# Weaving the top-k selection into the first half's query projection as well

## The chip, the cores and the metric

One core of one Trainium2 chip runs one layer of a streaming encoder in float32. The metric is the time of one execution on the device in microseconds (us). Engines in what follows: PE is TensorE (matmuls and transposes), DVE VectorE, ACT ScalarE, POOL GpSimd, SP the SyncE queue, which issues all the DMAs that this text speaks of.

## The reference, cut to what matters

The layer normalises 2048 prompt rows and 128 sample rows (17 tiles of 128 rows; tile 16 is the sample), multiplies them by one wide input matrix, and sends the columns to two mixers: a gated spatial mixer, and a sparse attention. For the sparse attention every query row first scores all keys with an indexer, keeps the 256 best, and attends to those alone:

```python
def _sparse_attend(q, qi, wi, q_pos, k, v, kidx, k_pos, topk):
    rel = jax.nn.relu(jnp.einsum('bqhd,bld->bqhl', qi, kidx) * (IDX_DIM ** -0.5))
    score = jnp.einsum('bqhl,bqh->bql', rel, wi).astype(jnp.float32) * (N_IDX_HEADS ** -0.5)
    score = jnp.where(_chunk_mask(q_pos, k_pos)[None], score, -jnp.inf)
    top_val, top_idx = lax.top_k(score, topk)
    ...
    p = jax.nn.softmax(logits, axis=-1).astype(v.dtype)
    out = jnp.einsum('bqhgn,bqnhd->bqhgd', p, v_sel)
```

The mixers' results are gated, projected, added to the input and normalised once more.

## The kernel before, in words

**Stages.** The 17 tiles are two halves, tiles 0 to 8 and 9 to 16, each of three groups of up to three tiles. The program goes through these stages:

1. `phase_p1(0)`: of half 0 the projections to keys, values and indexer keys (row by row, 128x292 matmuls), then to the indexer's queries (`C_QI`), then to the attention's queries (`C_Q`), both as 128x384 matmuls with the results stored to DRAM (`qi_s`, `q_s`, line 316).
2. `turn` of half 1 (normalised rows transposed into `hh` and `hl`), then `phase_p1(1)`, the same for half 1.
3. `phase_p2(1)`: the spatial mixer and the merge gates of half 1, and then, after the `turn` back, `phase_p2(0)` for half 0. Its last DVE instruction is a product at line 508.
4. `phase_b`: the attention, tile by tile from 0 to 15. DVE subtracts the penalty of unselected keys from the logits and takes the maximum (line 741), ACT takes the exponential, PE transposes, ACT and DVE split the transposed probabilities into two parts (lines 179 and 182), PE multiplies them with the values (line 780). Woven in at a low rate are the sample's attention (`attend_sample`, which takes over the selection's SBUF) and the first half of the merge (`merge_early`).
5. `phase_c`: the rest of the merge, the output projection and the last norm.

All float32 products are made of three products of a high and a low part (line 173), so PE has much to do everywhere; the weights' low part is a subtraction on POOL (line 182, `wl`).

**The selection.** `select(t, lane)` makes one tile's penalty. `scores` loads the tile's indexer queries (lines 518 and 519), multiplies them with the indexer keys on PE (lines 537 and 538), and adds up the eight heads on ACT and DVE (lines 540 to 544). A bisection over 31 bits then looks for the 256th score: each step counts how many of the tile's L scores are at least a candidate, in even and odd steps by turns on DVE (line 614) and on ACT as a sum of signs (line 624), and moves the candidate with two tiny DVE instructions (lines 625 or 629, and 630). At its end it goes over the scores in chunks of 512 (lines 656 to 663) and stores the penalty to DRAM (line 665). L is 128 times (t + 1): the last tiles are the dearest. Two lanes of tiles run beside each other, lane 0 with tiles 0, 1, 3, 5, 7, 9, 11, 13, 15 and lane 1 with 2, 4, 6, 8, 10, 16, 12, 14.

**What sets the order.** Each stage is a generator that yields the cost of what it has just emitted (`feats` yields 24 * n / 2400 for n columns). `weave(main, back, rate)` emits the main stage, and for each unit of cost lets `back` emit `rate` units: 0.95 for the selection in stages 2 and 3, 0.15 in `phase_b`. What is left of the selection is emitted at `drain(back)`, before the attention. The order in which each engine then gets its instructions is made when the program is built: a scheduler plays the program through and moves what it takes to be ready ahead of what it takes to be late, within the dependencies. On the chip each engine's list is fixed. The lines that call the stages:

```python
    drain(phase_p1(0, hT, p1, wa, lambda: nxt.ahead(4)))
    back = lanes(chain(select_all_of([0, 1]), *(select(t, 0) for t in (3, 5, 7, 9, 11, 13, 15))),
                 chain(*(select(t, 1) for t in (2, 4, 6, 8, 10, 16, 12, 14))))
    ...
    back = weave(phase_p1(1, hT, p1, wa), back, 0.95)
```

Of the kernel before, what the change touches and what calls it, by code (L numbers as in the profile page):

```python
# [36 lines left out]
C_U, C_V, C_ZA, C_Q, C_K, C_VV, C_ZB, C_QI, C_KI, C_WI, C_GA, C_GB = (  # L37
    0, 512, 1024, 1536, 2048, 2304, 2560, 3072, 3584, 3648, 3656, 4680)
# [3 lines left out]
GROUP_OF = {t: (g, i) for g, ts in enumerate(GROUPS) for i, t in enumerate(ts)}  # L42
# [15 lines left out]
def encoder_step(ctx: ExitStack, tc: tile.TileContext, x_prompt, x_sample, cache_k, cache_v, cache_kidx,  # L58
# [24 lines left out]
    class Banks:  # L83
# [4 lines left out]
        def set(self, **n):  # L88
            if self.pool:
                self.pool.close()  # L90
            self.n = n
            self.pool = Pool("ps_" + "_".join(n), space=bass.MemoryType.PSUM) if n else None
# [118 lines left out]
    def cols(c, n=256):  # L211
        return w_in[0][:, c:c + n]
# [60 lines left out]
    def phase_p1(half, hT, p1, wa, at_queries=None):  # L273

        gs = HALVES[half]
        gids = [GROUP_OF[g[0]][0] for g in gs]

        wb = load_w([cols(C_KI + 36, 36), cols(C_VV)], True)
        for gid, g in zip(gids, gs):
            k2s = []  # L280
            for i, t in enumerate(g):
                kk = p1.tile([P, 584], F32, tag="kk", name="kk", bufs=3)
                for j, w in enumerate((wa, wb)):
                    pk = bank("mm")
                    yield from rows(hT, pk[:, :292], t, w, 0, 292)
                    nc.scalar.activation(kk[:, 292 * j:292 * (j + 1)], pk[:, :292], AF.Copy)
                ST.dma_start(out_rows(o_k, s_k, t, "s h d -> s (h d)"), kk[:, :256])
                ST.dma_start(out_rows(o_ki, s_ki, t, None), kk[:, 256:320])
                ST.dma_start(out_rows(o_v, s_v, t, "s h d -> s (h d)"), kk[:, 328:])
                nc.vector.tensor_scalar(wiw[:, t, :], kk[:, 320:328], float(H ** -0.5) * 2.0 ** 24, None, op0=OP.mult)  # L290
                if t < NPT:
                    k2 = p1.tile([P, 2, HD], F32, tag="k2", name="k2", bufs=3)
                    nc.vector.tensor_copy(k2, kk[:, None, 256:320].to_broadcast([P, 2, HD]))
                    k2s.append(k2)
                else:
                    PS.dma_start(wi_s, wiw[:, t, :])
            m, c0 = len(k2s) * P, g[0] * P
            tp = bank("tr")
            for i, k2 in enumerate(k2s):
                nc.tensor.transpose(tp[:, i * P:(i + 1) * P], k2.rearrange("p a d -> p (a d)"), ident)  # L300
            split_hi(kist[:, c0:c0 + m], tp[:, :m])
            split_lo(kist[HD:, c0:c0 + m], tp[HD:, :m], kist[HD:, c0:c0 + m])
        for c, dst in ((C_QI, qi_s), (C_Q, q_s)):
            for b in range(2):
                if at_queries and c == C_Q and b:
                    at_queries()
                w = load_w([cols(c + 256 * b)])
                for j in range(2):
                    for gid in gids:
                        n = len(GROUPS[gid]) * P  # L310
                        pq = bank("mm")
                        yield from feats(hT, pq[:, :n], gid, w, j * P)
                        sb = p1.tile([P, 384], F32, tag="ev", name="ev", bufs=3)
                        nc.scalar.activation(sb[:, :n], pq[:, :n], AF.Copy)
                        r = (2 * b + j) * P
                        ST.dma_start(dst[gid][r:r + P, :], sb[:, :n])

    AT_FROM = 1

# [280 lines left out]

    def select(t, lane):

        keys = ("scores",) if t < NPT else ("scores", "mask")
        yield from take(*keys)
        s, L = yield from (scores(t) if t < NPT else scores_sample(lane))
# [28 lines left out]
        nxt = tk.tile([P, 1], F32, tag=f"bd{lane}", name="nxt")  # L634
# [427 lines left out]
    def chain(*gens):  # L1062
        for g in gens:
            yield from g
# [17 lines left out]
    def weave(main, back, rate):  # L1082

        due = 0.0
        for c in main:
            due += c * rate
            while due > 0.0 and back is not None:
                try:
                    due -= next(back)
                except StopIteration:  # L1090
                    back = None
        return back

    def drain(back):
        for _ in back or ():
            pass
# [4 lines left out]
    p1 = Pool("p1")  # L1101
    first = Normed(0, p1, 4).ahead(1)
    wa = load_w([cols(C_K), cols(C_KI, 36)], True, None, p1)
    hT = first.turn()
    nxt = Normed(1, p1, 4, first.gbc)
    drain(phase_p1(0, hT, p1, wa, lambda: nxt.ahead(4)))
    back = lanes(chain(select_all_of([0, 1]), *(select(t, 0) for t in (3, 5, 7, 9, 11, 13, 15))),
                 chain(*(select(t, 1) for t in (2, 4, 6, 8, 10, 16, 12, 14))))
    wa = load_w([cols(C_K), cols(C_KI, 36)], True)
    hT = nxt.turn()  # L1110
    back = weave(phase_p1(1, hT, p1, wa), back, 0.95)
# [8 lines left out]
    hT = px[1].turn()  # L1120
# [62 lines left out]
```

## Time and profile before

| | |
|---|---|
| three runs | 2234.58, 2236.76 and 2247.63 us, median 2236.76 us |
| profiled execution | 2242.49 us, of which the span from the first to the last instruction is 2240.7 us |
| granted PE clock, mean of the span | 0.978 of 2.4 GHz |
| busy share of the span | PE 96%, PE weight loads 91%, DVE 71%, ACT 54%, POOL 27% |
| stages in the span | `phase_p1(0)` to about 185 us, `phase_p1(1)` to 360, `phase_p2` to 1400, `phase_b` to 1986, `phase_c` to the end |
| selection | its first count starts at 203.3 us, its last chunk at 1555.6 us |

The busy time of PE is made of records whose ends are modelled, each longer than the distance to the next one, so a PE that shows as busy throughout can still be given more work in a stretch; the number of matmuls in a stretch is therefore read beside it. The granted clock of a stretch is 1.00 where the clock stood at 2.4 GHz throughout, and less where part of the stretch ran at 1.2 GHz.

### The profile page before, as it was taken

The page shows a single profiled execution, that of the slowest core. Times are in us where ns is not written, and L with a number is a line of the kernel's source. Part 1 is how long each engine was busy: PE and PEld are TensorE (multiplying, and loading weights), DVE is VectorE, ACT ScalarE, POOL GpSimd, SP SyncE. Part 2 cuts the span into 40 slices and gives each one's busy share as a digit, 9 for nine tenths or more (in the row PEclk, how much of TensorE's full clock was granted, in tenths as well). Part 3 has the DMA queues.
Part 4 walks back from the last instruction along what each step waited for, and adds up shares of the span by engine and source line. Part 5 has one row for each costly group of instructions (what it writes and reads, how often), then busy time and mean ns, then how long its engine had stood idle before and what let it go on. Part 6 is the DMA issues. An engine that isn't in the chain of part 4 may idle for free. (4 is left out here: it accounts for less than half of the span.)

```text
span 2240.7 us, 38226 instructions
## 1 busy us (share of the span) xinstructions
PE 2144.5 (96%) x13896; PEld 2030.0 (91%) x13896; DVE 1588.7 (71%) x4057; ACT 1215.8 (54%) x2181; POOL 594.8 (27%) x693
## 2 busy tenths in 40 slices
PE   8999999999999999999999999588999999998998
PEld 7999999999999998999999999577988999987886
DVE  7105857988897797856787678899788677755443
ACT  6225646565764655346664455776677666552221
POOL 1221222232432231222243221233212544333000
PEclk9999999999999999999999999699999999999999
DMA  6233233223432233112142211433332544244342
GB/s 209 80 109 114 82 96 95 68 67 87 129 105 83 73 108 104 48 59 90 40 136 85 82 56 54 118 80 89 92 79 53 145 122 117 88 153 145 130 160 76
DMA packets 251006, 218.83 MB, mean 98 GB/s; under 512 B 46529, under 2 KB 238657, under 8 KB 250817
## 3 DMA queue, kind: packets, MB, share of 16 engines
q1 hardware_dynamic: 250816, 216.39, 32.9%
q8 instruction: 109, 1.79, 0.3%
q14 instruction: 81, 0.66, 0.1%
HBM read 152.45 MB, written 63.81 MB: 97 GB/s over the span
## 5 line engine op out<-in xcount | busy, mean ns | idle before, releaser
L182 POOL TENSOR_TENSOR wl<-ws,wh 128x256 fp32r<-128x256 f32 (+1 forms) x376 | 310.7, 856 | 915.7 <-ACT wh L179 903.7
L624 ACT ACTIVATE junk<-s,bc 128x384 int8<-128x384 f32 (+14 forms) x232 | 294.0, 1268 | 185.5 <-DVE bc L630 184.0
L173 PE MATMUL ps_mm<-wh,hl 128*128 128x256 f32 (+1 forms) x1360 | 392.7, 289 | 0.9 <-DVE hl L182 0.9
L173 PE MATMUL ps_mm<-wh,hh 128*128 128x256 f32 (+1 forms) x1360 | 391.9, 289 | 1.5 <-ACT wh L179 0.7
L173 PE MATMUL ps_mm<-wl,hh 128*128 128x256 f32 (+1 forms) x1360 | 390.7, 287 | 0.3 <-POOL wl L182 0.3
L173 PE MATMUL ps_mm<-hh,wh 128*128 128x384 f32 (+1 forms) x1152 | 378.9, 329 | 2.4 <-ACT ev L474 2.4
L173 PE MATMUL ps_mm<-hl,wh 128*128 128x384 f32 (+1 forms) x1152 | 378.7, 329 | 0.0
L173 PE MATMUL ps_mm<-hh,wl 128*128 128x384 f32 (+1 forms) x1152 | 377.7, 329 | 0.0
L614 DVE TENSOR_SCALAR_CACHE_REDUCE junk<-s,bc 128x512 int8<-128x512 f32 (+14 forms) x248 | 351.9, 1421 | 5.2
L173 PEld LDWEIGHTS ps_mm<-wh,hh 128*128 128x128 f32 x1360 | 259.0, 191 | 6.1 <-issue 1.7
L173 PEld LDWEIGHTS ps_mm<-wh,hl 128*128 128x128 f32 x1360 | 259.1, 191 | 4.2 <-DVE hl L182 1.2
L173 PEld LDWEIGHTS ps_mm<-wl,hh 128*128 128x128 f32 x1360 | 259.3, 191 | 2.2 <-POOL wl L182 0.5
L544 DVE SCALAR_TENSOR_TENSOR s<-r,wiw,s 128x384 f32<-128x384 f32 (+2 forms) x266 | 201.5, 774 | 65.0 <-ACT r L540 64.2
L173 PEld LDWEIGHTS ps_mm<-hh,wh 128*128 128x128 f32 x1152 | 217.9, 189 | 4.6 <-ACT ev L474 2.8
L173 PEld LDWEIGHTS ps_mm<-hl,wh 128*128 128x128 f32 x1152 | 217.7, 189 | 2.1
L173 PEld LDWEIGHTS ps_mm<-hh,wl 128*128 128x128 f32 x1152 | 217.8, 189 | 1.8
L540 ACT ACTIVATE r<-ps_ix 128x512 f32<-128x512 f32 (+2 forms) x304 | 157.2, 538 | 111.3 <-PE ps_ix L538 104.7
L763 PE MATMUL ps_tr<-ident,sx 128*128 128x128 f32 x1088 | 177.0, 281 | 14.8 <-ACT sx L746 4.3
L780 PE MATMUL ps_po<-pth,vst 128*128 128x256 f32 x544 | 161.7, 313 | 9.3 <-ACT osb L784 8.8
L182 DVE TENSOR_TENSOR ptl<-ps_tr,pth 128x512 fp32r<-128x512 f32 (+1 forms) x231 | 149.6, 658 | 28.7 <-ACT pth L179 27.7
L179 ACT ACTIVATE pth<-ps_tr 128x512 fp32r<-128x512 f32 (+1 forms) x231 | 127.6, 572 | 76.4 <-PE ps_tr L763 69.7
L746 ACT ACTIVATE sx<-sx,mx 128x128 f32<-128x128 f32 (+15 forms) x128 | 153.6, 1201 | 20.6 <-DVE mx L745 20.2
(287 smaller groups left out, 4572.7 us busy)
## 6 DMA issues: line engine op xcount, KB each, us to landing
ws<-in_w_in_dram SPq DMA_DIRECT2D x88, 512.0 KB, 3.9
x<-in_x_prompt_dram SPq DMA_DIRECT2D x41, 512.0 KB, 3.6
q<-q_s SPq DMA_DIRECT2D x34, 256.0 KB, 4.4
out_dram<-x SPq DMA_DIRECT2D x17, 512.0 KB, 2.6
gb_s<-ev SPq DMA_DIRECT2D x40, 192.0 KB, 2.5
ma_s<-ev SPq DMA_DIRECT2D x40, 192.0 KB, 1.9
ma<-ma_s SPq DMA_DIRECT2D x40, 192.0 KB, 3.3
sg<-gb_s SPq DMA_DIRECT2D x40, 192.0 KB, 2.4
```

The costliest lines, as they stand in the source:

```text
L173: nc.tensor.matmul(out, a(k), b(k), start=(n == 0), stop=(n == 3 * nk - 1))
L179: nc.scalar.activation(dst, src, AF.Copy)
L182: (eng or nc.vector).tensor_tensor(dst, src, hi.bitcast(F32), op=OP.subtract)
L540: nc.scalar.activation(r[:, :n], pi[:, :n], AF.Relu, scale=HD ** -0.5)
L544: nc.vector.scalar_tensor_tensor(s[:, c:c + n], r[:, :n], wiw[:, t, h:h + 1], s[:, c:c + n], op0=OP.mult, op1=OP.add)
L614: nc.vector.tensor_scalar(junk[:, :L], s[:, :L], thr, 0.0, op0=op, op1=OP.add, accum_out=cnt)
L624: nc.scalar.activation(junk[:, :L], s[:, :L], AF.Sign, bias=candf, scale=-1.0, accum_out=cnt)
L746: nc.scalar.activation(sx, sx, AF.Exp, bias=mx[:, 7:8], scale=HD ** -0.5, accum_out=T.rsum[:, h:h + 1])
L763: nc.tensor.transpose(tv[:, l, hh * P:(hh + 1) * P], pr[hh][:, (l0 + l) * P:(l0 + l + 1) * P], ident)
L780: nc.tensor.matmul(po, vst[:, l0 + l, n, :], pp[:, l, :], start=(l0 + l == 0 and i == 0), stop=(l0 + l == t and i == 1))
```

## The change

The selection's generator is made before `phase_p1(0)` instead of after it, and that stage is woven with it at 0.95 too. `weave` gives `back` no turn until some indexer queries have been emitted in full: at the end of the `C_QI` block the half's three groups enter `asked`, and until `asked` holds something nothing is due. A tile whose group is not yet in `asked` waits in `select`, each turn of waiting counted as 0.5. Nothing else is changed, and the same instructions are issued. From line 318 on the lines of the changed kernel are five higher than before, from line 603 on seven.

```diff
                         r = (2 * b + j) * P
                         ST.dma_start(dst[gid][r:r + P, :], sb[:, :n])
+            if c == C_QI:
+                asked.update(gids)
+
+
+    asked = set()
 
     AT_FROM = 1
...
     def select(t, lane):
 
+        while GROUP_OF[t][0] not in asked:
+            yield 0.5
         keys = ("scores",) if t < NPT else ("scores", "mask")
...
         due = 0.0
         for c in main:
-            due += c * rate
+            due += c * rate if asked else 0.0
             while due > 0.0 and back is not None:
...
     nxt = Normed(1, p1, 4, first.gbc)
-    drain(phase_p1(0, hT, p1, wa, lambda: nxt.ahead(4)))
     back = lanes(chain(select_all_of([0, 1]), *(select(t, 0) for t in (3, 5, 7, 9, 11, 13, 15))),
                  chain(*(select(t, 1) for t in (2, 4, 6, 8, 10, 16, 12, 14))))
+    back = weave(phase_p1(0, hT, p1, wa, lambda: nxt.ahead(4)), back, 0.95)
     wa = load_w([cols(C_K), cols(C_KI, 36)], True)
```

How it moves instructions is seen at two places. The first is DVE where the projections end, from the last product of `phase_p2(0)` (line 508 before, 513 in the changed kernel). Before, the list goes on like this (`bn` is the count, `bg` and `bc` the step and the candidate, `eq`, `pre` and `pen` the chunks, 128x1920 the scores of tile 14):

```order
L508 TENSOR_TENSOR ev<-ev,ps_mm 128x384
L659 COPY bl<-pre 128x1
L661 SCALAR_TENSOR_TENSOR eq<-pre,bd,eq 128x512
L625 TENSOR_SCALAR bg<-bn 128x1
L663 SCALAR_TENSOR_TENSOR pen<-junk,eq 128x512
L630 SCALAR_TENSOR_TENSOR bc<-bg,bc 128x1
L656 TENSOR_SCALAR eq<-s,bc 128x512
L614 TENSOR_SCALAR junk,bn<-s,bc 128x1920
L657 SCALAR_TENSOR_TENSOR pre<-eq,bl 128x512
L629 TENSOR_SCALAR bg<-bn 128x1
```

The changed kernel's DVE list at the same place, where `kst` and `q` are already the attention's first keys and queries:

```order
L513 TENSOR_TENSOR ev<-ev,ps_mm 128x384
L636 TENSOR_SCALAR bg<-bn 128x1
L637 SCALAR_TENSOR_TENSOR bc<-bg,bc 128x1
L632 TENSOR_SCALAR bg<-bn 128x1
L637 SCALAR_TENSOR_TENSOR bc<-bg,bc 128x1
L621 TENSOR_SCALAR junk,bn<-s,bc 128x1920
L636 TENSOR_SCALAR bg<-bn 128x1
L637 SCALAR_TENSOR_TENSOR bc<-bg,bc 128x1
L632 TENSOR_SCALAR bg<-bn 128x1
L637 SCALAR_TENSOR_TENSOR bc<-bg,bc 128x1
L621 TENSOR_SCALAR junk,bn<-s,bc 128x1920
L182 TENSOR_TENSOR kst<-ps_tr,kst 64x4x128
```

Tile 15's last chunks no longer stand there. Counted to the end of the selection, 88 DVE instructions of the selection come behind that product before and 52 in the changed kernel: of the counts 12 and 6, of the steps 20 and 9, of the chunks 6 and 4; on ACT 10 sums of signs and 4. The last chunk stands behind 79 of the attention's subtractions of line 741 before, behind 45 in the changed kernel.

The second place is the SP queue in `phase_p1(0)`, where the `C_Q` results (`q_s`, three groups) are stored and the next stage's weights (`ws`) are loaded. Before:

```order
L316 DMA q_s_80<-ev 128x384
L316 DMA q_s_78<-ev 128x384
L316 DMA q_s_79<-ev 128x384
L316 DMA q_s_80<-ev 128x384
L157 DMA ws<-in_w_in_dram 128x4x256
L316 DMA q_s_78<-ev 128x384
L157 DMA ws<-in_w_in_dram 128x4x36
L316 DMA q_s_79<-ev 128x384
L157 DMA ws<-in_w_in_dram 128x4x36
L316 DMA q_s_80<-ev 128x384
L157 DMA ws<-in_w_in_dram 128x4x256
L316 DMA q_s_78<-ev 128x384
```

In the changed kernel, a little further on in the same stage:

```order
L316 DMA q_s_78<-ev 128x384
L316 DMA q_s_79<-ev 128x384
L157 DMA ws<-in_w_in_dram 128x4x36
L157 DMA ws<-in_w_in_dram 128x4x256
L523 DMA qi<-qi_s_85 64x8x128
L524 DMA qi<-qi_s_85 64x8x128
L316 DMA q_s_80<-ev 128x384
L316 DMA q_s_78<-ev 128x384
L316 DMA q_s_79<-ev 128x384
L228 DMA x<-in_x_prompt_dram 128x1024
L316 DMA q_s_80<-ev 128x384
```

The indexer queries of tiles 3 and 4 are now loaded between the stores of `C_Q`; before, the queue carried one such load there, that of tile 2 ahead of the `C_Q` stores, and the next came in `phase_p1(1)`. On PE the first product of line 537 moves from the row numbered 1045 to the row numbered 758, into `C_Q` of half 0, and the last from 8587 to 8372.

## Rows read from the trace of the kernel before

**Rows 1.** The page: busy time of each engine, and two rows of 40 slices.
```profile
PE 2144.5 (96%) x13896; PEld 2030.0 (91%) x13896; DVE 1588.7 (71%) x4057; ACT 1215.8 (54%) x2181; POOL 594.8 (27%) x693
...
PE   8999999999999999999999999588999999998998
...
PEclk9999999999999999999999999699999999999999
```

**Rows 2.** Windows: length, busy PE, PEld, DVE, ACT, POOL (instructions), clock, DMA share, GB/s.
```profile
80.00:160.00 80.00, 80.00 (x467) 79.96 (x466) 2.57 (x4) 18.26 (x30) 23.64 (x34) 1.00 0.36 106
...
280.00:300.00 20.00, 17.44 (x93) 17.11 (x93) 10.71 (x24) 7.19 (x16) 7.12 (x8) 0.83 0.38 111
...
320.00:340.00 20.00, 20.00 (x127) 20.00 (x126) 13.54 (x44) 11.62 (x26) 3.16 (x5) 1.00 0.23 70
...
800.00:880.00 80.00, 75.26 (x505) 70.47 (x504) 67.47 (x149) 40.67 (x61) 18.61 (x23) 0.96 0.38 116
...
1280.00:1360.00 80.00, 80.00 (x447) 78.41 (x446) 62.14 (x114) 45.47 (x69) 16.25 (x20) 1.00 0.23 67
...
1600.00:1760.00 160.00, 157.13 (x1091) 141.72 (x1090) 129.14 (x385) 115.23 (x222) 42.10 (x45) 0.99 0.31 78
```

**Rows 3.** Windows at the attention's start.
```profile
1400.00:1411.00 11.00, 1.59 (x7) 1.25 (x8) 9.57 (x19) 4.15 (x6) 1.16 (x1) 0.58 0.77 186
...
1411.00:1498.00 87.00, 65.77 (x377) 58.01 (x375) 74.72 (x249) 69.79 (x166) 26.48 (x28) 0.78 0.36 90
1498.00:1560.00 62.00, 52.53 (x355) 47.44 (x354) 58.73 (x168) 39.63 (x82) 15.16 (x14) 0.94 0.29 74
```

**Rows 4.** Windows of line 614 (DVE) and line 624 (ACT), accumulator reads included.
```profile
1400.00:1560.00 160.00, 26.59 (x24) 0.83 0.36 90
...
1400.00:1560.00 160.00, 17.82 (x18) 0.83 0.36 90
```

**Rows 5.** DVE's groups from 1411 to 1560: busy, mean ns | idle before.
```profile
L614 DVE TENSOR_SCALAR_CACHE_REDUCE junk<-s,bc 128x1920 int8<-128x1920 f32 x9 | 19.9, 2208 | 0.1
...
L630 DVE SCALAR_TENSOR_TENSOR bc<-bg,bc 128x1 int32<-128x1 int32 x17 | 6.1, 358 | 0.1
...
L661 DVE SCALAR_TENSOR_TENSOR eq<-pre,bd,eq 128x512 f32<-128x512 f32 x3 | 3.1, 1037 | 0.0
L657 DVE TENSOR_TENSOR_SCAN pre<-eq,bl 128x512 f32<-128x512 f32 x2 | 2.6, 1276 | 0.0
...
L663 DVE SCALAR_TENSOR_TENSOR pen<-junk,eq 128x512 bf16<-128x512 int8 x3 | 2.0, 678 | 0.0
L656 DVE TENSOR_SCALAR eq<-s,bc 128x512 f32<-128x512 f32 x3 | 1.4, 477 | 0.0
L629 DVE TENSOR_SCALAR bg<-bn 128x1 int32<-128x1 f32 x9 | 1.3, 147 | 0.1
```

**Rows 6.** PE's longest wait from 1400 to 1560: us in total, times, longest.
```profile
PE ps_tr L699 <- DMA kk<-out_dram: 11.5, 2, 7.1
```

**Rows 7.** Timeline of DVE: 45th subtraction, next count, the selection's last chunk.
```profile
1492.06 0.56 DVE L741 CUSTOM_DVE_ANT_0 sx<-ps_mm,pen 128x384 f32<-128x384 f32 x1
...
1493.03 2.21 DVE L614 TENSOR_SCALAR_CACHE_REDUCE junk<-s,bc 128x1920 int8<-128x1920 f32 x1
...
1555.57 0.56 DVE L663 SCALAR_TENSOR_TENSOR pen<-junk,eq 128x384 bf16<-128x384 int8 x1
```

**Rows 8.** Timeline of PE: the stalls near the selection's start, idle in brackets.
```profile
208.44 0.50 PE L537 MATMUL ps_ix<-kist,qih 128*128 128x512 f32 x1 [2.52 <-ACT qih L179]
...
293.07 0.69 PE L537 MATMUL ps_ix<-kist,qih 128*128 128x384 f32 x1 [2.56 <-ACT r L540]
```

**Rows 9.** POOL's weight splits: 80 to 130 (ns min/median/max), then 260 to 360.
```profile
L182 POOL TENSOR_TENSOR wl<-ws,wh x24: 727/737/751, 80.1 to 121.8; 128x256 fp32r<-128x256 f32 x24
...
L182 POOL TENSOR_TENSOR wl<-ws,wh 128x256 fp32r<-128x256 f32 x34 | 27.0, 823 | 59.6 <-ACT wh L179 59.6
```

**Rows 10.** Waits of the SP queue over the span: total, times, longest.
```profile
SPq L518 <- PE ps_ix L538: 33.5, 9, 17.5
```

## The prediction

> **What bounds the kernel now.** I read the page first [rows 1]. PE is busy for 96% of the span, no other engine for more than 71%, and the row of slices has one hole: the 26th slice (1400 to 1456 us) shows 5 tenths, the two behind it 8. The granted clock falls to 0.6 in the same slice. So nearly all of the kernel waits for PE, whose work this change doesn't touch, and what can be won lies in that hole.
>
> The windows show how the stages differ. In the projections PE is full, whether the selection runs beside them or not (80 to 160 us without it, 320 to 340 and 1280 to 1360 with it) [rows 2]. In the steady attention it is full too: 157.1 of 160 us with 1091 matmuls, DVE at 129.1 (1600 to 1760) [rows 2]. Only at the attention's start is DVE the fuller engine [rows 3]: 58.7 of 62 us (95%) from 1498 to 1560, where PE has 52.5, and 74.7 of 87 from 1411 to 1498, where PE has 65.8. The first 11 us there are something else: PE waits for the first keys [rows 6], and DVE is busy with leftover selection.
>
> That selection ends at 1556 us [rows 7], 156 us after the projections, and it sits in the same in-order DVE list as the attention's subtractions. From 1400 to 1560 its counts take 26.6 us of DVE and its sign sums 17.8 us of ACT [rows 4], and beside the counts stand steps and chunks [rows 5]. So this is the stage to price.
>
> **The change, part by part.** All instructions stay; they move.
>
> *Start in the first half.* The 12 products of half 0's `C_Q` yield 24 * 384 / 2400 = 3.84 each, 46.1 in all, so the selection is emitted 0.95 * 46.1 = 44 units sooner. In time it is 12 * 24 = 288 matmuls at 80 us / 460 = 174 ns (nearly all the 467 records of that window are these): 50 us [rows 2]. DVE was busy for 2.6 of 80 us there and ACT for 18.3, so the work fits beside PE. PE's own part of it (lines 537 and 538) is only moved: what it adds in this stage it takes from later ones, and its sum is zero, since PE is full in both. No tile waits for `asked` later: summing the yields, half 1's `C_QI` is out after 127 units of selection, and lane 0 comes to tile 9, the first of that half, after 237.
>
> *New stalls, or stalls that go.* The selection's start costs PE something now: 2.52 us idle at 208, 2.56 us at 293 with the clock at 0.83 over 20 us (another 3.4 us) [rows 2, 8]. That is 8.5 us that may vanish, since DVE and ACT are emptier where it starts now. On the other side, the `turn` of half 1 had DVE and ACT nearly to itself and now meets counts. The nearest row is the second `turn`, inside the woven selection: 4.7 us idle and a clock of 0.96 (3.2 us), 8 us (800 to 880) [rows 2]. Between -8.5 and +8 I take 0: one is as near as the other.
>
> *POOL.* A weight split takes 737 ns while DVE is idle and 823 ns beside the selection [rows 9]. Some 24 splits come in the newly woven stretch (eight for the last `C_Q` weights, eight for each of the next two): 24 * 86 ns = 2 us. POOL is busy for 30% there [rows 2], so this is covered by its idle time; without that cover it is 2 us. The Trainium skill (GPSIMD Engine Reference, Key points) has GpSimd share its SBUF interfaces with VectorE, in contention above all with two-input DVE instructions. By that rule alone the change would cost these 2 us; the trace agrees on the contention (737 against 823 ns).
>
> *The end of the projections.* By the changed order, 6 counts, 11 steps and 2 chunks of DVE leave the attention's start, and 6 sign sums of ACT. In DVE time [rows 5]: 6 * 2.29 (2.21 and the accumulator read of some 0.08) = 13.7; 11 * (0.147 + 0.358) = 5.6; 2 * (0.48 + 1.28 + 1.04 + 0.68 + 0.14 for the carry) = 7.2; together 26.5 us. In ACT time 6 * 17.8 / 9 = 11.9 us [rows 4]. Not all of this is on the path, and the order says where it isn't. The selection now ends behind the 45th subtraction instead of the 79th. The 45th starts at 1492 us [rows 7]. Up to there, the changed list still holds about 4 counts, 4 chunks and some steps once two counts have gone by while PE waits for keys (4 * 2.29 + 4 * 3.6 + 5 = 29 us), as much DVE time as the 8 counts and their steps before (26 us). So before 1498 I take nothing, with bounds of -10 (some five sign sums of 1.98 us leave ACT, if it is ACT that binds there) and +3 (the 29 against the 26).
>
> Behind the 45th subtraction the selection is gone. Up to 1560 that frees two counts with their steps, the one at 1493 too, and four chunks: 3 * 2.29 + 4 * 3.6 = 21 us of DVE, the most that can be saved. What remains is PE's: 355 matmuls at the steady attention's rate (160 us / 1091 = 147 ns) need 52 us in place of 62, a saving of 10. The busy time gives the same: 52.5 us at a clock of 0.94 is 49.4 at full clock and fills 50.4 us at the steady 98%, a saving of 11.6 [rows 2, 3]. PE is the engine that takes over as the bound, so between 10 and 21 I take 12. The attention behind it stays full on PE, so the 12 us reach the end. What is late next is PE itself.
>
> *What starts sooner.* The sample's attention takes over the selection's memory and comes forward with it, as does the early merge; both are PE work that fills the same list. The attention's last tiles then run for longer without the merge beside them; PE is full there as in the steady attention, so nothing is added.
>
> **Sum.** -12 + 0 + 0 = -12 us. The profiled execution, 2242.5 us (2240.7 of span), becomes 2230.5. It lay 5.7 us above the median of the runs, 2236.8, so I forecast 2225 us, 0.5% less. Ends of the terms together: -21 - 8.5 - 10 = -39.5, and on the other side 8 + 3 + 2 = +13, or, with the 10 us of PE's row kept, +3.
>
> **Rivals.**
>
> 1. *The whole stretch loosens (more is won).* If the 10 sign sums and 12 counts made the start slow from 1411 on, not only behind 1492, the start runs at the steady rate: 732 matmuls (377 + 355) at 147 ns are 107.6 us, and the low clock up to 1498 (0.78 over 87 us) leaves, say, 12 of its 19 us: 120 in place of 149, -29, so 2208 us. For it speaks that ACT was at 80% there as well. Against it: up to 1492 DVE keeps as much work.
>
> 2. *Nothing is won.* The start may be bound by its own chains (small tiles: logits, maximum, exponential, transposes), by the low clock up to 1498, and by the keys' loads [rows 3, 6], none of which is touched. Then the DVE time that leaves turns into idle time: 2237, give or take 5. The Trainium skill (Perfetto Trace Analysis, Identifying the Most-Contended Engine) has one work on the engine with the highest occupancy first. Over the whole span that is PE [rows 1], which keeps its work, and by this rule the time would stay at 2237. Against it speaks that DVE is at 95% from 1498 on while PE is not full.
>
> 3. *Slower: the SP queue is held up in `phase_p1(0)`.* The loads of indexer queries of tiles 3 and 4 now stand in that in-order queue between the stores of `C_Q` and the next weights, and each waits until the tile ahead of it has used the one buffer of queries. Such a wait has lasted up to 17.5 us [rows 10]. Behind it wait the stores, so the three result buffers, so ACT's evictions, so PE's banks. Three buffers cover 3 * 24 * 174 ns = 12.5 us, and from there the wait decides: 5 us of stall, and 3.4 us for the clock, 8.4 us at each place. With the loads of tiles 2, 3 and 4 and the `turn` behind them that is up to 34 us, net of the gain +21, so 2258; from the second place on the change loses. Against it: half 1's `C_Q`, woven in the same manner with the same loads in its queue, runs with a full PE (320 to 340) [rows 2].
>
> **How the numbers follow.** Forecast (2219 to 2231) 0.50, the first rival (2203 to 2218) 0.24, the second (2232 to 2242) 0.18, the third (2243 to 2260) 0.08. The predicted time is 2225. The range leaves out the farther half of the first rival's low end and most of the third: 2207 to 2243. About 1% (22 us) is what a measurement of this kernel can tell from no change: faster by more (under 2214) is two thirds of the first rival and the tails, 0.20; slower by more (over 2259) is the third rival's end, 0.04; within it 0.76.
>
> **What would show it.** In the profile of the changed kernel: the first counts at about 150 to 160 us instead of 203; PE full from there to the end of `phase_p1(1)`; the projections' end again at about 1400, within 8 us; the selection's last chunk at 1485 to 1500; behind that DVE under 85% and PE at 98%; the attention's end about 12 us earlier. A start that ends over 20 us sooner shows the first rival, a DVE that idles beside an idle PE the second, PE waiting for weights or for banks before 215 us the third. The forecast is wrong if the projections end more than 8 us from 1400, or if the saving appears and is given back behind 1560, in the sample's attention or in the merge.

## The result, and the profile after

The changed kernel takes 2208.99 us (median of four runs, 2207.11 to 2215.95) where the kernel before, timed beside it, takes 2237.74 (2234.58 to 2247.63): a ratio of 0.987, 95% interval 0.983 to 0.991, 1.3% or 28.7 us faster. The forecast was 2225, with 0.76 on a change within 1%; what came lies in the range, near its low end, and among the cases that had 0.20. The profiled execution took 2210.12 us with a span of 2208.1, 32.6 us less than the span before; the sums below are made against that. One execution of each kernel was profiled, and the kernel before varies by 13 us from execution to execution, so a difference of a few us in one stretch is not told from that spread by one pair of profiles; the two large ones below are borne out by the kernels of the experiments.

The page of the changed kernel answers to [rows 1]: the same hole in the row of slices, one tenth less deep (5 tenths before, 6 now), and shorter: 8 and 9 behind it instead of 8 and 8.

```profile
PE 2131.6 (97%) x13896; PEld 2018.2 (91%) x13896; DVE 1586.7 (72%) x4057; ACT 1217.2 (55%) x2181; POOL 591.1 (27%) x693
...
PE   8999999999999998999999999689999999999998
...
PEclk9999999999999999999999999799999999999999
```

The selection's first count starts at 151.84 us instead of 203.3, and its last chunk lies just behind the 45th subtraction (DVE's timeline: start, us, engine, line; compare [rows 7], where the 45th had started at 1492.06 and the last chunk at 1555.57):

```profile
1479.25 0.55 DVE L748 CUSTOM_DVE_ANT_0 sx<-ps_mm,pen 128x384 f32<-128x384 f32 x1
...
1480.33 0.55 DVE L670 SCALAR_TENSOR_TENSOR pen<-junk,eq 128x384 bf16<-128x384 int8 x1
```

Where the 32.6 us come from can be read off four marks in DVE's list that both kernels have: the last product (line 513, before 508), the 45th and 79th subtraction and the 318th (lines 748 and 741).

| stretch | before, us | after, us | difference |
|---|---|---|---|
| start to the last product | 1398.78 | 1389.61 | -9.2 |
| last product to 45th subtraction | 93.28 | 89.64 | -3.6 |
| 45th to 79th | 62.97 | 49.36 | -13.6 |
| 79th to 318th | 413.10 | 408.56 | -4.5 |
| 318th to the end | 272.57 | 270.93 | -1.6 |

First, the projections. Two windows around the old stalls [rows 8], of the kernel before and then of the changed one (columns as in [rows 2]):

```profile
180.00:215.00 35.00, 32.48 (x234) 31.79 (x233) 24.08 (x64) 21.96 (x46) 7.42 (x8) 1.00 0.49 140
260.00:310.00 50.00, 47.22 (x282) 46.26 (x281) 31.86 (x93) 20.09 (x44) 14.99 (x20) 0.93 0.36 108
```

```profile
180.00:215.00 35.00, 34.88 (x246) 34.26 (x245) 30.06 (x140) 27.09 (x64) 6.32 (x8) 1.00 0.47 143
260.00:310.00 50.00, 48.25 (x301) 47.52 (x301) 37.19 (x133) 31.62 (x66) 15.24 (x21) 1.00 0.39 109
```

PE loses 0.1 us instead of 2.5 in the first window, and in the second the clock stays up: 31 more matmuls in the same 85 us, although DVE and ACT have more to do there.

Then the attention's head, in the windows of the changed kernel that answer to [rows 3]:

```profile
1400.00:1411.00 11.00, 6.21 (x26) 5.14 (x25) 8.74 (x33) 6.82 (x14) 1.46 (x2) 0.50 0.59 139
1411.00:1479.00 68.00, 55.45 (x343) 48.98 (x341) 63.64 (x206) 51.34 (x137) 23.60 (x26) 0.86 0.39 99
1479.00:1528.00 49.00, 46.25 (x335) 42.38 (x336) 41.60 (x142) 38.87 (x85) 15.05 (x21) 1.00 0.56 135
```

Behind the 45th subtraction DVE falls from 95% to 85%, PE rises from 85% to 94%, and the clock from 0.94 to 1.00. Ahead of it DVE is at 94% (63.64 of 68), fuller than before (74.72 of 87, 86%) [rows 3].

### The profile page after: what moved, and what is told of

The parts are those of the page before. It is cut to its first block, busy times and chain, and to the rows that moved or that the text cites. A ratio compares the mean times of both kernels' runs of the same rounds, so it can differ in the third digit from the quotient of the medians.

```text
span 2208.1 us, 38238 instructions
## 1 busy us (share of the span) xinstructions
PE 2131.6 (97%) x13896; PEld 2018.2 (91%) x13896; DVE 1586.7 (72%) x4057; ACT 1217.2 (55%) x2181; POOL 591.1 (27%) x693
## 4 chain that ended last, share of the span: by engine, by line
PE 80%; DMA 7%; DVE 6%; ACT 3%; issue 2%; POOL 1%; SPq 1%; ACTq 0%; DVEq 0%; POOLq 0%
PE ps_mm L173 54%; PE ps_po L787 5%; PE ps_tr L770 4%; PE ps_ix L542 3%; PE ps_ix L543 2%; PE ps_mm L746 2%; PE ps_mm L747 2%; PE ps_ix L173 2%; DMA ws<-in_w_in_dram 1%; DVE junk L621 1%; DMA q<-q_s 1%; POOL wl L182 1%; PE ps_mm L798 1%; DMA bl<-bt_s 1%; DMA qi<-qi_s 1%
## 5 line engine op out<-in xcount | busy, mean ns | idle before, releaser
L182 POOL TENSOR_TENSOR wl<-ws,wh 128x256 fp32r<-128x256 f32 (+1 forms) x376 | 303.3, 837 | 923.3 <-ACT wh L179 906.1
L621 DVE TENSOR_SCALAR_CACHE_REDUCE junk<-s,bc 128x640 int8<-128x640 f32 (+14 forms) x248 | 351.8, 1421 | 5.3
L770 PE MATMUL ps_tr<-ident,sx 128*128 128x128 f32 x1088 | 172.0, 276 | 7.2 <-ACT sx L753 5.7
```

The costliest lines, as they stand in the source:

```text
L182: (eng or nc.vector).tensor_tensor(dst, src, hi.bitcast(F32), op=OP.subtract)
L621: nc.vector.tensor_scalar(junk[:, :L], s[:, :L], thr, 0.0, op0=op, op1=OP.add, accum_out=cnt)
L770: nc.tensor.transpose(tv[:, l, hh * P:(hh + 1) * P], pr[hh][:, (l0 + l) * P:(l0 + l + 1) * P], ident)
```

## The experiments

**First theory**: two gains that add up, some 9 us in the projections from stalls that go with the early start, and the rest at the attention's head because less selection (the tail) stands in the lists there. The rivals: all of it comes from the one, or all from the other.

**e1, the short tail alone** (late start; eight steps of one tile left out):

```diff
-        for b in range(30, -1, -1):
+        for b in range(30, -1 if t != 14 else 7, -1):
```

> The head alone: the kernel before, with the selection started late as it was, and the last 8 of the 31 bisection steps of tile 14 left out (so that tile's selection is coarser), which leaves 68 instead of 88 selection rows in DVE's list behind the projections and 48 instead of 79 subtractions ahead of the last chunk (the change: 52 and 45). Theory (two gains that add up, about 10 us in the projections from stalls that go with the early start, and 14 to 17 us at the attention's head from the shorter tail): the last product stays at 1397 to 1400 us, the attention's end comes 10 to 17 us sooner, 2223 us, ratio 0.990 to 0.996. Rival (the tail costs nothing by itself, all is won by the earlier start): 2237 us, ratio 1.000. Second rival (all is won by the shorter tail): 2212, ratio 0.988.

Measured: 2224.63 us, ratio 0.993 (0.991 to 0.995). The last product stays at 1397.4; from there to the 318th subtraction it takes 557.1 us instead of 569.4. The head's gain exists without the early start, though this kernel also does less; e5 and e6 below shorten the tail without that.

**e2, the early start alone** (the tail made long again by passes that move the candidate by nothing):

```diff
+        for b in range(10 if t == 14 else 0):
+            if b % 2:
+                nc.scalar.activation(junk[:, :L], s[:, :L], AF.Sign, bias=candf, scale=-1.0, accum_out=cnt)
+                nc.vector.tensor_scalar(g, cnt, float(L - 2 * TOPK + 1), 0.0, op0=OP.is_gt, op1=OP.mult)
...
+            else:
+                yield count(candf, OP.is_ge)
+                nc.vector.tensor_scalar(g, cnt, TOPK - 0.5, 0.0, op0=OP.is_lt, op1=OP.mult)
+            nc.vector.scalar_tensor_tensor(cand, g, 0, cand, op0=OP.bitwise_xor, op1=OP.bitwise_xor)
```

> The early start alone: the changed kernel, with 10 more passes of tile 14 that change nothing of its result, so that 11 counts and 9 sign sums stand behind the projections and 77 subtractions ahead of the last chunk, nearly as in the kernel before (12, 10 and 79). Theory (two gains): the last product at 1390 us as in the changed kernel, the head as slow as before, 2225 us, ratio 0.993 to 0.997. Rival (all from the shorter tail): 2237, ratio 1.000. Second rival (all from the early start): 2209, ratio 0.987.

Measured: 2242.62 us, ratio 1.001 (0.9995 to 1.0025). The theory's 2225 is missed by 18 us, and the number is that of the first rival, but not for its reason. The last product is at 1389.57, so the 9 us are there, and the 79th subtraction starts 20.0 us sooner than before. All of it is lost again behind: 433.8 us from the 79th to the 318th. The windows between those marks (last product to 79th, 79th to 318th), first of the kernel before, then of e2:

```profile
1398.78:1555.03 156.25, 114.92 (x697) 102.01 (x698) 139.56 (x421) 111.50 (x247) 42.80 (x43) 0.83 0.35 87
1555.03:1968.13 413.10, 406.67 (x2815) 375.66 (x2814) 320.22 (x910) 280.08 (x500) 144.08 (x155) 0.99 0.37 101
```

```profile
1389.57:1535.06 145.49, 112.06 (x695) 96.72 (x696) 132.85 (x406) 109.71 (x244) 38.23 (x43) 0.87 0.35 91
1535.06:1968.85 433.79, 414.03 (x2818) 380.16 (x2817) 319.80 (x909) 282.51 (x500) 144.26 (x154) 0.97 0.36 97
```

The same matmuls (2818 and 2815) leave PE idle for 19.8 us there instead of 6.4, at a clock of 0.97 instead of 0.99. e12 asks whether that belongs to the long tail.

**e12, the same with eight added passes:**

```diff
-        for b in range(10 if t == 14 else 0):
+        for b in range(8 if t == 14 else 0):
```

> As the early start with 10 added passes of tile 14, which took 2243 us, but with 8 (10 counts and 8 sign sums behind the projections, 67 subtractions ahead of the last chunk), to see whether that kernel's slow attention (434 us from the 79th to the 318th subtraction, against 413 before) belongs to the length of its tail or to that one built order. By the tail's length: 558 to 568 us from the last product to the 318th subtraction, last product at 1390, time 2220 to 2230. If added passes behind an early start cost more than the same tail behind a late one: 572 or more, 2234 to 2243.

Measured: 2219.02 us, ratio 0.991 (0.988 to 0.994); last product 1388.9, 554.3 us to the 318th, 414.8 of them behind the 79th, with 4.7 us of idle PE. So an early start with a tail of 67 subtractions doesn't have e2's slow attention. What makes it in e2, with 77, stays open: e10 and e11 below, with a late start and 71 and 97, idle there for 16.2 and 18.4 us too, and the kernel before, with 79, for only 6.4. Neither the tail's length nor the built order is singled out by these kernels. Against e8 below, a late start with nearly the same tail (69), e12 ends its projections 6.2 us sooner and is 13 us faster (e8 is one run).

**e3, early start, no tail** (20 steps of tile 14 left out; the diff is e1's with 19 for 7):

> The changed kernel with the last 20 bisection steps of tile 14 left out (a coarser selection for that tile), so that no selection stands behind the projections. Theory (what is left of the selection, 6 counts, 9 steps and 4 chunks of DVE, some 33 us, still holds the head back while PE is at 80% there): 6 to 12 us less than the changed kernel, 2197 to 2203 us, ratio 0.982 to 0.985. Rival (what is left of the head's loss is the clock and the keys' loads): 2207 to 2210, ratio 0.987.

Measured: 2189.59 us, ratio 0.978 (0.974 to 0.981), 19 us below the changed kernel where 6 to 12 were expected. The projections end at 1388.4, so nearly all of it is attention: 528.1 us to the 318th instead of 547.6. Between these marks DVE is busy for 25.7 us less (409.4 instead of 435.1), so the tail costs 19.5 us for 25.7 us of DVE time, far more than was expected but not more than its busy time.

**e4 and e7, the early start at other paces** (0.95 became 1.05 and 1.0 in the four calls):

```diff
-    back = weave(phase_p1(0, hT, p1, wa, lambda: nxt.ahead(4)), back, 0.95)
+    back = weave(phase_p1(0, hT, p1, wa, lambda: nxt.ahead(4)), back, 1.05)
```

> The changed kernel with the pace 1.05 in place of 0.95 in the projections: 37 instead of 52 selection rows in DVE's list behind the projections, 25 instead of 45 subtractions ahead of the last chunk, the same work. Theory: the tail's 15 rows less (3 counts, 6 steps, 3 sign sums) are worth 2 to 5 us, 2204 to 2207, ratio 0.984 to 0.987, with the last product at 1390. Rival (the head is bound by clock and keys): 2209, ratio 0.987 to 0.988. Second rival (the faster pace brings stalls into the projections): last product at 1393 or later, 2212.

> The changed kernel with the pace 1.0 instead of 0.95, with the same 52 rows of tail, for where its projections end. Theory A (the early start itself takes away the stalls at the selection's start): last product at 1388 to 1392 us and the time at 2205 to 2213. Theory C (the projections' 9 us are an accident of one built order, as pace 1.05 with its last product at 1398 suggests): anywhere between 1390 and 1400.

Measured: e4 2213.36 us, ratio 0.988 (0.985 to 0.991), e7 2217.55 (one run). Their last products are at 1398.0 and 1397.1: the projections' gain is nearly gone, although both start early. That is what e4's second rival named (1393 or later), and in e7 it lies outside theory A (1388 to 1392) and inside theory C's wide range. The stretch from the last product to the 318th is 541.8 us in e4 (25 subtractions ahead of the last chunk) and 547.0 in e7, the changed kernel's 547.6 with the changed kernel's tail. In e4 PE idles for 4.2 us from 185 to 360 and for 6.3 from 360 to 800, mostly in front of score matmuls; in the changed kernel it is 1.9 and 0.1.

**e5 and e6, the tail cut without leaving anything out**, by selecting the sample's tile 16, whose passes are short, behind tile 14; in e5 on the changed kernel, in e6 on the kernel before:

```diff
-                 chain(*(select(t, 1) for t in (2, 4, 6, 8, 10, 16, 12, 14))))
+                 chain(*(select(t, 1) for t in (2, 4, 6, 8, 10, 12, 14, 16))))
```

> The changed kernel with tile 16 (the sample's, whose passes are short) selected behind tile 14 instead of ahead of tile 12 in lane 1: the same work, and by the built order no selection is left behind the projections (52 rows before). Theory (the tail is what costs at the head; the kernel whose tail was cut short by leaving steps out took 2190 us): 2187 to 2196 us, ratio 0.975 to 0.982. Rival (that kernel was faster because it did less, not because its tail was gone): 2204 to 2210, ratio 0.986 to 0.988.

> The kernel before with the same new place for tile 16, so a late start with all its work and a tail of 20 rows (3 counts, 2 steps, one chunk, one sign sum), with no subtraction behind it. Theory A (two gains that add up): the tail's gain without the projections' 9 us, the last product at 1397 to 1400 us, 2196 to 2206 us, ratio 0.981 to 0.986, and 7 to 12 us slower than the early start with the same place. Theory B (the early start is worth only the tail that it shortens; what the projections win is given back behind them): within 3 us of the early start with the same place, 2187 to 2196.

Measured: e5 2183.64 us, ratio 0.975 (0.973 to 0.977), the fastest kernel of this study; e6 2196.21, ratio 0.982 (0.978 to 0.985). With next to no tail in either, the early start is still worth 12.6 us, and it lies where theory A has it: the last products are at 1385.0 and 1396.3, 11.3 us apart (e6's is just below theory A's 1397, and the 12.6 just above its 12). What a missing tail does is seen in the windows between the marks, of the changed kernel and then of e5:

```profile
1389.61:1528.61 139.00, 109.97 (x709) 98.08 (x709) 120.28 (x390) 103.74 (x243) 40.85 (x50) 0.86 0.49 120
1528.61:1937.17 408.56, 401.26 (x2804) 370.89 (x2803) 314.86 (x893) 278.17 (x491) 142.91 (x148) 1.00 0.34 94
```

```profile
1385.01:1521.54 136.53, 124.21 (x807) 106.81 (x805) 102.67 (x373) 103.95 (x267) 37.70 (x42) 0.94 0.49 120
1521.54:1908.73 387.19, 379.31 (x2705) 356.38 (x2704) 307.26 (x855) 268.12 (x458) 142.29 (x148) 1.00 0.33 93
```

PE does 98 more matmuls up to the 79th subtraction in 2.5 us less, and has 99 fewer left behind it. The sample's attention takes over the selection's memory and so can't start before the last chunk; of its 152 matmuls 32 start ahead of the 79th subtraction in the changed kernel and 133 in e5, which covers the whole of that difference. Its first transposes, of the kernel before and then of e5 (first and last start behind the durations):

```profile
L901 PE MATMUL ps_ix<-ident,kc x32: 270/272/421, 1568.1 to 1713.7; 128*128 128x128 f32 x32
```

```profile
L908 PE MATMUL ps_ix<-ident,kc x32: 271/273/448, 1384.8 to 1529.5; 128*128 128x128 f32 x32
```

In e5 it begins with the attention and fills PE where PE waits for DVE and ACT: 12.3 us idle in that stretch, against 29.0 in the changed kernel and 41.3 before. No run takes the tail away and still holds the sample's attention back, so how much the DVE time that goes with the tail (75% busy there instead of 87%) brings by itself is not shown.

**e8 and e9, the other side of the start.** e8 is the late start at pace 1.03 (0.95 in three calls before). e9 starts later still, in `C_Q` of half 1:

```diff
-            if c == C_QI:
-                asked.update(gids)
+            if c == C_QI and half == 1:
+                asked.update(GROUP_OF[t][0] for t in GROUP_OF)
```

> The kernel before (late start) with the pace 1.03, 86 rows of tail instead of 88, for where its projections end. Theory A: the stalls behind the start stay, last product at 1397 to 1401 us, time 2230 to 2240. Theory C: anywhere between 1390 and 1405.

> The changed kernel with the selection's start moved the other way, to where the indexer queries of half 1 are out (in that half's C_Q products; DVE is empty there, as it is in half 0's). By the built order 264 selection rows are left behind the projections and 149 subtractions ahead of the last chunk. Theory D (the stalls at the start come from meeting the K, V and KI stage, where ACT and DVE have evictions and splits of their own): from 180 to 360 us PE idles under 2.5 us at a clock of 1.00 (late start: 5 to 9 us at 0.97 to 0.99). Theory E (the selection's first tiles cost PE their stalls wherever it starts): 5 us or more there. For the attention, by 0.55 us for each subtraction ahead of the last chunk (528 us from the last product to the 318th subtraction with none, 569 with 79): about 605 to 615 us, and 2265 to 2285 us in all. If the tail only costs up to the 79th subtraction: 570 to 580, and 2240 to 2250.

Measured: e8 2232.37 us, last product 1395.1 (one run), 2 us short of theory A's range, in theory C's; e9 2305.51 (one run), last product 1376.7, 636.7 us to the 318th. The windows from 185 to 360 us, of e8 and then of e9:

```profile
185.00:360.00 175.00, 165.63 (x1083) 163.64 (x1082) 131.87 (x456) 101.45 (x227) 38.32 (x47) 0.97 0.34 99
```

```profile
185.00:360.00 175.00, 174.23 (x1215) 173.31 (x1214) 77.16 (x272) 76.69 (x163) 42.43 (x56) 1.00 0.36 103
```

Theory D holds for this stretch: PE idles for 0.8 us there when the selection begins in half 1's `C_Q`, for 5.3 to 9.4 us in the six kernels that begin with the K, V and KI stage of half 1, and for 1.6 to 5.0 in the seven that begin in half 0's `C_Q` (1.6 to 2.6 at pace 0.95; e4 and e7, at the faster paces, have 4.2 and 5.0). Each of those six has the stall of [rows 8] on the same score matmul at 208 to 210 us, 2.5 to 3.7 us long. In e9 the selection is there only from 297 us on, and from 360 to 800 PE idles for 4.2 us, against 0.1 in the changed kernel. e9's attention costs more than either figure expected: its tail is 264 rows, and 80 of the 608 score matmuls too are left behind the projections, which is also why its last product comes so early.

**e10 and e11, DVE or ACT.** In the kernel before, the last 16 passes of tile 14 all go to one engine (each run has one of the two lines with +):

```diff
-        return b % 2 == lane
+        return b % 2 == lane or (L == 15 * P and b < 16)      # e10: sign sums on ACT
+        return b % 2 == lane and (L != 15 * P or b >= 16)     # e11: counts on DVE
```

> The kernel before with the last 16 passes of tile 14 all as sign sums on ACT: behind the projections 4 counts and 18 sign sums instead of 12 and 10, 71 instead of 79 subtractions ahead of the last chunk. If DVE is what binds at the attention's head: from the last product to the 79th subtraction 140 to 150 us (before: 156), time 2222 to 2232. If ACT binds as much or more: 156 to 170, time 2238 to 2252.

> The kernel before with the last 16 passes of tile 14 all as counts on DVE: 20 counts and 2 sign sums instead of 12 and 10, 97 subtractions ahead of the last chunk. If DVE binds at the attention's head: from the last product to the 79th subtraction 165 to 176 us (before: 156), time 2247 to 2262. If ACT binds: 145 to 155, time 2225 to 2237.

Measured: 2248.27 and 2249.13 us (one run each). From the last product to the 79th subtraction (e10, then e11):

```profile
1394.91:1548.75 153.84, 113.23 (x678) 97.37 (x678) 122.54 (x404) 122.85 (x258) 41.50 (x45) 0.83 0.39 95
```

```profile
1393.86:1545.43 151.57, 110.19 (x699) 95.59 (x699) 140.77 (x420) 96.71 (x229) 39.97 (x43) 0.88 0.36 88
```

DVE's share goes from 80% to 93% and ACT's from 80% to 64%, and the two stretches lie within 3 us of each other (156.25 in the kernel before), with 41 us of idle PE in both. Neither theory holds in full: e10's stretch lies between the two ranges and its time in ACT's, e11's stretch in ACT's range and its time in DVE's. So neither engine's busy time alone sets the head. What these kernels and the kernel before share is the selection's late end (1541, 1584 and 1556 us), and with it the late start of the sample's attention; that this is the cause is argued, not shown. Their whole attention takes 579 us instead of 569, and that loss lies behind the 79th subtraction (to the 318th; e10, then e11), where the kernel before takes 413.1 us with 6.4 us of idle PE:

```profile
1548.75:1973.82 425.07, 408.89 (x2833) 374.94 (x2833) 320.28 (x911) 284.26 (x505) 144.88 (x154) 1.00 0.34 96
```

```profile
1545.43:1972.84 427.41, 409.04 (x2809) 375.46 (x2810) 328.60 (x926) 282.22 (x499) 143.68 (x151) 0.99 0.34 95
```

All kernels in one table; the attention is the time from the last product to the 318th subtraction:

| kernel | start | subtractions ahead of the last chunk | last product | attention | median time |
|---|---|---|---|---|---|
| e9 | later | 149 | 1376.7 | 636.7 | 2305.5 |
| e11 | late | 97 | 1393.9 | 579.0 | 2249.1 |
| before | late | 79 | 1398.8 | 569.4 | 2237.7 |
| e2 | early | 77 | 1389.6 | 579.3 | 2242.6 |
| e10 | late | 71 | 1394.9 | 578.9 | 2248.3 |
| e8 | late | 69 | 1395.1 | 566.7 | 2232.4 |
| e12 | early | 67 | 1388.9 | 554.3 | 2219.0 |
| e1 | late | 48 | 1397.4 | 557.1 | 2224.6 |
| after | early | 45 | 1389.6 | 547.6 | 2209.0 |
| e7 | early | 45 | 1397.1 | 547.0 | 2217.6 |
| e4 | early | 25 | 1398.0 | 541.8 | 2213.4 |
| e3, e5 | early | 0 | 1388.4, 1385.0 | 528.1, 523.7 | 2189.6, 2183.6 |
| e6 | late | 0 | 1396.3 | 528.8 | 2196.2 |

From 0 to 79 subtractions the attention grows by about 43 us, some 0.54 us for each; e2 and e10 lie 11 to 14 us above that line, e12 lies 9 below it, and e9 with its 149 some 29 above, so it is a trend and no law. The changed kernel moves along it from 79 to 45 and takes 9 us off the projections.

## Why the prediction came out as it did

**The head behind the 45th subtraction: right.** Forecast -12, measured -13.6, and in the way described: DVE at 85%, PE at the steady rate (339 matmuls in 49.4 us, 146 ns each; the forecast used 147). Of the 13.6 us the rate accounts for 11; the rest comes from the 18 matmuls fewer that stand in this stretch (357 before). PE is at 94% there and not at the 98% that was named. The clock, which was part of the -12, gave all it could, from 0.94 to 1.00.

**Up to the 45th: taken as 0 with bounds of -10 and +3, measured -3.6.** Inside the bounds. Of this, 2.5 us came from the keys: PE's longest wait is 9.0 us instead of 11.5 [rows 6].

```profile
PE ps_tr L706 <- DMA kk<-out_dram: 9.0, 2, 5.1
PE ps_tr L770 <- ACT sx L753: 5.7, 6, 1.7
PE ps_po L787 <- ACT osb L791: 5.3, 5, 2.2
PE ps_mm L746 <- DVE mx L748: 3.6, 2, 2.7
```

These are PE's waits from 1390 to 1560 in the changed kernel (total, times, longest). With the keys aside they are spread over ACT and DVE, which agrees with e10 and e11.

**The step that failed: "New stalls, or stalls that go".** It was taken as 0 between -8.5 and +8, "one is as near as the other". The projections ended 9.2 us sooner, just past the low bound, and by the prediction's own condition (more than 8 us from 1400) the forecast was wrong there. The two stalls that were priced, 2.52 + 2.56 us of idle PE and 3.4 us of clock, did go, but the 9.2 us are not these 8.5. Over the whole of the projections PE idles for 21.7 us instead of 28.5, and the same 9148 matmuls keep it busy for 2.4 us less at a higher clock (before, then changed):

```profile
0.00:1398.78 1398.78, 1370.31 (x9148) 1335.78 (x9148) 1007.69 (x2480) 751.40 (x1304) 363.17 (x442) 0.99 0.31 90
```

```profile
0.00:1389.61 1389.61, 1367.92 (x9148) 1333.15 (x9148) 1031.73 (x2521) 762.58 (x1315) 360.40 (x442) 1.00 0.31 91
```

Half of those 6.8 us of idle time lies around the old start, from 185 to 360 us (before, then changed; stalls of 0.5 and 1.3 us are left there, at 284 and 294):

```profile
185.00:360.00 175.00, 169.70 (x1124) 167.56 (x1123) 134.45 (x465) 102.82 (x232) 37.97 (x48) 0.98 0.34 100
```

```profile
185.00:360.00 175.00, 173.13 (x1158) 170.97 (x1157) 144.38 (x506) 108.22 (x240) 37.22 (x48) 1.00 0.34 100
```

The other half is the balance of small stalls further on, which the prediction had not priced: 0.1 us instead of 2.7 from 360 to 800, and 2.7 us less behind 900. For the priced half the reason to take the gain was missing. Those two stalls were waits for ACT (`qih` and `r`) in the stage in which ACT and DVE also evict and split keys and values, and the selection was being moved to a stage that the same rows showed as empty (DVE 2.6 of 80 us [rows 2]). The cost on the other side, the `turn` of half 1, didn't come: PE is full from 180 to 215. In the second `turn`, which was the model for it, PE idles for 5.1 of the 80 us where [rows 2] had 4.7, and up to 900 us for 7.1 instead of 5.0 (the row from 1600 belongs to the next step):

```profile
800.00:880.00 80.00, 74.89 (x502) 69.05 (x501) 53.29 (x113) 27.31 (x47) 17.19 (x22) 0.98 0.40 119
...
1600.00:1760.00 160.00, 153.60 (x1056) 140.18 (x1055) 119.49 (x342) 109.19 (x198) 61.18 (x61) 0.99 0.38 106
```

But -8.5 would not have been safe either: e4 and e7 start early too and end their projections at 1397 to 1398. The gain belongs to the early start at pace 0.95, and was seen in two built orders (the changed kernel's, whose projections e2, e3 and e12 nearly share, and e5's); the six late kernels end theirs at 1393.9 to 1398.8. Which rule ties the pace to the stalls stays open.

**What starts sooner: the saving is not given back here, but the step was too simple.** "PE is full there as in the steady attention, so nothing is added" was taken for the sample's attention and the merge. From the 79th subtraction on the changed kernel gains another 4.5 us: the clock loss of the kernel before (0.99 over 406.67 us of busy PE, some 4 us) is mostly gone, and 11 of the matmuls are already done. The row from 1600 to 1760 above has 6.4 us of idle PE where [rows 2] had 2.9; the sample's attention, which that row held before, has largely gone by. And e3 and e5 show a price that the prediction didn't have: the tail also keeps 98 matmuls out of a stretch in which PE has gaps.

**The rivals.** The first gave 2208, and 2209 was measured, but not by its mechanism: a start that loosens as a whole would have shown between the last product and the 45th subtraction, and 3.6 of the 32.6 us lie there. By the sign that the prediction named for it, a start that ends over 20 us sooner, it would seem to have come (the 79th subtraction at 1528.6 instead of 1555.0), but 9.2 of those 26.4 us are the projections'. The range reached down to 2207 for this rival's sake, so that the measured time lies in it is partly luck. The second had PE idle instead of DVE, at 2237; behind the 45th subtraction PE's share rose instead. The Trainium skill (Perfetto Trace Analysis, Identifying the Most-Contended Engine) has one work on the engine with the highest occupancy first, and judges TensorE by its MFU and the busy share of its weight loads, not by its matmuls' busy time. Over the span of the kernel before, PE comes first by the weight loads (91%) as by the matmuls (96%); the next is DVE with 71%. Its work didn't change and 1.3% was won nevertheless, so taken over the whole span the rule does not point to this gain. Taken by stage, the head's row (DVE 95%, PE 85%) had pointed the right way for the last 62 us of it. The third rival didn't come: the wait exists, and PE is full all the same. SP's wait over the span and PE's window of the newly woven stretch:

```profile
SPq L523 <- PE ps_ix L543: 23.3, 6, 17.2
```

```profile
130.00:180.00 50.00, 50.00 (x282) 49.32 (x281) 28.44 (x82) 24.38 (x50) 13.54 (x16) 1.00 0.40 110
```

**POOL: right.** The weight splits of the stretch from 130 to 260 us take 877 ns instead of the 737 of an idle DVE [rows 9], and nothing waits for them beyond 0.3 us of PE's weight loads. The prediction's "above all with two-input DVE instructions" says more than the section of the Trainium skill that it names, which puts these beside one other kind. Which DVE instructions lengthen the splits, no run here shows.

```profile
L182 POOL TENSOR_TENSOR wl<-ws,wh 128x256 fp32r<-128x256 f32 x12 | 10.2, 877 | 65.8 <-ACT wh L179 65.8
...
PEld ps_mm L173 <- POOL wl L182: 0.3, 1, 0.3
```

## What to carry to other kernels

Background work that is left in the in-order lists when a stage begins costs there, even where DVE is not full over the stage (79% from the last product to the 318th subtraction): here three quarters to nearly all of its DVE time (19.5 us for 25.7 from the changed kernel to e3, 23.8 for 25.2 to e5, 40.6 for 43.7 from the kernel before to e6). It also keeps out whatever needs its memory, here 98 matmuls that went into PE's gaps once the tail was gone. Look at the last chain of such work first: putting a short piece last won 45 us with the late start, more than starting everything 50 us sooner (29), and some 25 us on top of the early start (57 for both together). And when a start moves, take the stalls at the old place as a gain if the rows name a busy engine there and an empty one at the new place, but check the pace, which can bring others.

## What the runs showed of the hardware that was not expected

At the head, moving sixteen passes of some 2 us each from ACT (e10, DVE and ACT both 80% busy) to DVE (e11, 93% and 64%) moved the stretch by less than 3 us out of 154: with three engines handing small tiles round, the share of one engine was no measure of what its relief brings. And the granted clock (a mean over stretches at its two levels, 1.2 and 2.4 GHz) goes with the idle time of PE, though loosely: between the last product and the 79th subtraction it was 0.83 with 41.3 us idle (before), 0.86 with 29.0 (after), 0.91 with 15.3 (e6) and 0.94 with 12.3 (e5), but also 0.83 with 33.7 (e1) and 0.88 with 41.4 (e11). As an estimate from these rows, the clock took (156.25 - 41.3) * 0.17 = 19.5 us before and 124.2 * 0.06 = 7.5 in e5, so 12 us for 29 us of idle time, 0.4 for each; from e11 (110.2 * 0.12 = 13.2) to e5 it is 0.2.
